# Retention outputs by features: centred values as stationary operand, and a group norm from a spread sum of squares

## The chip, the cores and the metric

The kernel runs on one core of one Trainium2 chip, as one launch. The metric is the time of that core on the device in microseconds (us), here the median of three runs. TensorE (PE in the rows; PEld is its weight load) multiplies, VectorE (DVE) and ScalarE (ACT) work on single elements, GpSimd (POOL) and SyncE (SP) mostly issue transfers. Each engine works through its own queue in order and waits for the others by semaphores.

## The reference, cut to what matters

A trunk of 4 layers is applied to 256 prompt frames and 64 sample frames, in float32. Each layer is FFN, token mixer, FFN. The mixer of layers 0 and 3 is retention, with 4 heads, 256 features of query and key and 512 of value per head. Per chunk of 64 frames:

```python
inner = einsum('bhid,bhjd->bhij', qc, kc) * decay
o = einsum('bhij,bhje->bhie', inner, vc) + einsum('bhid,bhde->bhie', qc * q_dec, s)
s = s * c_dec + einsum('bhjd,bhje->bhde', kc * k_dec, vc)
...
mu = mean(o, axis=-1)
var = mean(square(o - mu), axis=-1)
o = (o - mu) * rsqrt(var + EPS) * gn_g
y = (silu(g) * o) @ w_out
```

The final state of both sequences is an output. Only the sample has a state to begin with; the prompt's 256 frames are taken in one triangular product here, without a state.

## The kernel before, in words

**Weights and clock of the program.** All weights stream from memory as [128, 1024] chunks of eight [128, 128] tiles. ScalarE makes the high part of a chunk (`hi`, L274) and VectorE the low part (`lo`, L281), three chunks ahead of use; each tile is then used by three TensorE products of 320 or 322 columns (L375 to L377, the main products). Everything else is woven in by ticks: a tick comes every four tiles, that is every 12 main products. `at(delay, f)` records the work of `f` that many ticks later, and a heap keeps the order. A chunk border is every second tick, and `split_hi` is recorded at a border ahead of the work of that tick. So the order on every engine is fixed when the program is built.

**A head of retention** (L650 to L810) takes 24 ticks: two columns each of q, k, v, v, g, g, eight tiles a column. `normed` (L590) takes a pair of columns out of the products' memory on VectorE, `shifted` (L596) adds the shift on ScalarE, `rotate` (L668 to L673) turns q and k. Then come steps between the weight tiles: `k_rows` (L685) and `v_rows` (L696) turn k and v to rows of tokens, `scores` (L705) multiplies k by q, `attend` (L721) multiplies three tiles of tokens with 512 columns of values, the sample's with the state `s0` and 64 rows of tokens; `bn_stats` and `bn_aggr` read mean and variance there. `group_norm` waits for the three, makes 1/sqrt and scales the rows on ScalarE (`on`, L736). `gate` (L743, L747) turns a tile of 128 features back to features by tokens, multiplies by the gate and the gain and splits the product into two parts (L401, L402). `state_prompt` (L754, L756) and `state_sample` (L764, L767) make the new states, which leave on POOL's queue through three `st` buffers; on the same queue, behind them, the next head's state is loaded (L782).

**Pools that set waits.** The steps share three banks of TensorE's output memory (`wk`), taken in turn. `wide` has two buffers. The mixer's output projection (`out_projection`, L807 on) takes 16 operands; its first four outputs take the first nine operands (`RET_EARLY`) before the rest. Each output that is done is added to x by VectorE (`residual`, L555), which then prepares the next sub-layer's operand (L496, L502, L508, L513). The output banks are two tiles of two banks; output 4 takes the tile of outputs 0 and 2, so that it waits for both residuals.

Between the retention heads VectorE also works on the modulation vectors (`junk`, L472, two products of 1.2 us for a unit), by a plan that is not changed.

Of the kernel before, what the change touches and what calls it, by code (L numbers as in the profile page):

```python
# [19 lines left out]
P = 128  # L20
# [5 lines left out]
TOKT = ((0, 128), (128, 256), (256, 320))  # L26
NB = NT + 2
# [18 lines left out]
# Work on the modulation vectors per chunk of weights: row tiles on the tensor engine at a time, and units that the  # L46
# vector engine takes (before and in a sub-layer's output projection; in a retention head, by chunk).
# [4 lines left out]
# Chunks that are split ahead, buffers.  # L52
# [13 lines left out]
def sub_tiles(kind, layer):  # L66
    """[128, 128] weight tiles of a sub-layer, (weight, index, row tile, first column), as they are used."""
# [92 lines left out]
def ada_layout(subs):  # L160
    """Vector -> which engine computes it."""
# [3 lines left out]
class Consts:  # L165
    """Columns of the array of constants."""
# [25 lines left out]
def tables():  # L192
# [12 lines left out]
                   g[:, :, 0] ** np.maximum(63 - np.arange(P)[:, None], 0)], axis=2) / 16.0  # L205
# [5 lines left out]
def windows():  # L211
    """[rows, windows, tokens out]: trailing means less the frame, for the three row tiles of a projection."""
# [19 lines left out]
class Stream:  # L232
    """Weights in the order of their use: loaded ahead, split into two float32r parts ahead."""
# [76 lines left out]
class Kernel:  # L310
# [75 lines left out]
    def four_banks(self):  # L386
        """Neighbours are in different tiles."""
# [9 lines left out]
    def parts(self, src):  # L397
        """Two float32r parts of a [128, 320] operand."""
# [6 lines left out]
    def parts_later(self, src, done):  # L405
        """The same, the second part a tick later."""
# [10 lines left out]
    def rsqrt(self, m, n):  # L417
        """1 / sqrt(m) of a [128, n] operand in full float32."""
# [13 lines left out]
    def at(self, delay, f):  # L432
        """Traces f between the weight tiles, `delay` ticks of four tiles from now."""
# [58 lines left out]
    def operand_hi(self, n, t):  # L492
        """Tile t of x times the gain of sub-layer n, in two parts."""
# [27 lines left out]
    def rstd(self, cols):  # L521
        """1 / rms of the tokens, by tokens, for three sets of 128 columns."""
# [7 lines left out]
    def begin(self):  # L530
        """Queues the norm of the sub-layer that starts."""
# [54 lines left out]
    def normed(self, ps):  # L586
        """Two projections with the norm of the tokens; the shifts' part is in the last two columns."""
# [48 lines left out]
    def retention(self, n, layer):  # L636
        nc, a, j = self.nc, self.a, layer // 3
        with self.tc.tile_pool(name=f"ret{n}", bufs=2) as rp:
            y1 = [None] * (4 * RH)
            self.begin()  # L640
            for h in range(RH):
                self.retention_head(rp, j, h, y1)
# [563 lines left out]
```

## Time and profile before

| what | value |
|---|---|
| median of three runs | 2764.23 us (2763.4 to 2764.54) |
| profiled execution, span from its first to its last instruction | 2763.1 us |
| what the runs have beyond that span | 1.1 us |
| busy: TensorE, VectorE, ScalarE | 99 %, 77 %, 48 % |
| granted TensorE clock, mean | 0.999 |
| retention of layer 0, main products by L375 to L377 with what is woven in | about 278 to 577 us |
| retention of layer 3 | about 2225 to 2523 us |

The span is the time from the first to the last instruction of one execution. Busy time is a union of intervals; products of TensorE overlap in the records, so that the time which one of them takes away from the queue is the distance between starts, and not its duration. A row of a timeline gives the start and the length of a run of equal instructions, a row of groups the mean of one.

### The profile page before, as it was taken

Reading aid. Unit: us, or ns where it says so; the run is one execution under the profiler, and the core shown is the slowest. Engines: PE = TensorE matmul, PEld = TensorE weight load, DVE = VectorE, ACT = ScalarE, POOL = GpSimd, SP = SyncE. Lnnn points to the kernel's source line nnn. Section 1 sums busy time; section 2 is a strip of 40 time slices with the busy share of each in tenths; the row PEclk is TensorE's granted clock in tenths of the full one; section 3 lists DMA queues with packets and bytes.
Section 4 is the critical chain, followed back from the end, with each engine's and each line's share of the span. In section 5 each row is a group of like instructions: output and inputs, shape, how many; then the busy total and the mean of one; then the engine's idle time right before and its main releaser. Section 6 shows DMA issues by size and latency. Waiting matters only on the chain. (4 is left out here: it accounts for less than half of the span.)

```text
span 2763.1 us, 46811 instructions
## 1 busy us (share of the span) xinstructions
PE 2730.5 (99%) x18328; PEld 2614.3 (95%) x18328; DVE 2129.9 (77%) x3614; ACT 1335.3 (48%) x2409; POOL 63.7 (2%) x117
## 2 busy tenths in 40 slices
PE   7999999999999999999999999999999999999999
PEld 5999988899999998999999988999999998889999
DVE  5888777788888888889788776788888877756553
ACT  4554444445535544554454455555455445444552
POOL 0000000000000002000000021000000000000000
PEclk9999999999999999999999999999999999999999
DMA  8667454566666674667566543466666654444442
GB/s 329 234 220 243 169 177 158 205 216 216 218 223 214 211 234 161 226 217 238 193 218 224 198 154 118 167 214 211 224 203 210 226 178 166 165 141 153 150 151 94
DMA packets 149852, 543.63 MB, mean 197 GB/s; under 512 B 17744, under 2 KB 19024, under 8 KB 149376
## 3 DMA queue, kind: packets, MB, share of 16 engines
q1 hardware_dynamic: 142272, 517.51, 54.8%
q0 software_dynamic: 6208, 21.82, 2.3%
q8 instruction: 144, 2.36, 0.4%
q10 hardware_dynamic: 1152, 1.31, 0.1%
q14 instruction: 76, 0.62, 0.1%
HBM read 528.13 MB, written 12.44 MB: 196 GB/s over the span
## 5 line engine op out<-in xcount | busy, mean ns | idle before, releaser
L375 PE MATMUL mm<-xh,hi 128*128 128x322 f32 x3776 | 1196.6, 317 | 3.0 <-DVE xt L555 1.2
L377 PE MATMUL mm<-xh,lo 128*128 128x322 f32 x3776 | 1174.8, 311 | 0.0
L376 PE MATMUL mm<-xl,hi 128*128 128x322 f32 x3776 | 1171.5, 310 | 0.1
L274 ACT ACTIVATE hi<-raw 128x1024 fp32r<-128x1024 f32 x690 | 727.2, 1057 | 760.5 <-PE mm L376 652.2
L281 DVE TENSOR_TENSOR lo<-raw,hi 128x1024 fp32r<-128x1024 f32 x690 | 840.8, 1222 | 251.1 <-ACT hi L274 239.2
L375 PEld LDWEIGHTS mm<-xh,hi 128*128 128x128 f32 x3776 | 713.7, 189 | 32.9 <-issue 25.0
L376 PEld LDWEIGHTS mm<-xl,hi 128*128 128x128 f32 x3776 | 713.7, 189 | 3.2 <-issue 2.9
L377 PEld LDWEIGHTS mm<-xh,lo 128*128 128x128 f32 x3776 | 710.3, 188 | 0.0
L472 DVE SCALAR_TENSOR_TENSOR junk<-raw,cb 128x1024 f32<-128x1024 f32 x480 | 586.4, 1222 | 8.6
L375 PE MATMUL mm<-part,hi 128*128 128x320 f32 x1728 | 539.4, 312 | 1.9 <-DVE xt L555 1.9
L376 PE MATMUL mm<-part,hi 128*128 128x320 f32 x1728 | 536.7, 311 | 0.1
L377 PE MATMUL mm<-part,lo 128*128 128x320 f32 x1728 | 536.4, 310 | 0.0
L596 ACT ACTIVATE twin<-twin 128x256 f32<-128x256 f32 (+1 forms) x944 | 328.9, 419 | 184.8 <-DVE twin L590 184.5
L375 PEld LDWEIGHTS mm<-part,hi 128*128 128x128 f32 x1728 | 327.5, 190 | 8.9 <-issue 4.9
L376 PEld LDWEIGHTS mm<-part,hi 128*128 128x128 f32 x1728 | 325.6, 188 | 1.3 <-issue 1.0
L377 PEld LDWEIGHTS mm<-part,lo 128*128 128x128 f32 x1728 | 325.6, 188 | 0.0
L590 DVE TENSOR_TENSOR twin<-mm,rx 128x644 f32<-128x644 f32 (+1 forms) x240 | 195.2, 814 | 85.0 <-PE mm L377 84.5
L496 ACT ACTIVATE xh<-xt,mod 128x256 fp32r<-128x256 f32 x192 | 71.2, 421 | 197.7 <-DVE xt L555 196.1
L555 DVE SCALAR_TENSOR_TENSOR xt<-mm,mod,xt 128x256 f32<-128x256 f32 (+1 forms) x176 | 59.3, 378 | 62.5 <-PE mm L377 62.4
L409 ACT ACTIVATE part<-twin 128x320 fp32r<-128x320 f32 x176 | 81.2, 461 | 48.0 <-DVE twin L611 48.0
L611 DVE TENSOR_TENSOR twin<-twin 128x320 f32<-128x320 f32 x176 | 85.9, 491 | 23.2 <-ACT twin L596 18.7
L412 DVE TENSOR_TENSOR part<-twin,part 128x320 fp32r<-128x320 f32 x176 | 85.5, 486 | 1.1 <-ACT part L409 1.1
(165 smaller groups left out, 1146.8 us busy)
## 6 DMA issues: line engine op xcount, KB each, us to landing
raw<-in_wmain SPq DMA_DIRECT2D x690, 512.0 KB, 3.7
raw<-in_wada SPq DMA_DIRECT2D x288, 512.0 KB, 4.2
out_ret_p<-st POOLq DMA_DIRECT2D x16, 256.0 KB, 2.3
out_ret_s<-st POOLq DMA_DIRECT2D x16, 256.0 KB, 3.9
s<-in_s POOLq DMA_DIRECT2D x6, 512.0 KB, 7.0
fb<-in_fb POOLq DMA_DIRECT2D x8, 384.0 KB, 4.2
xt<-in_xt SPq DMA_DIRECT2D x1, 1280.0 KB, 11.3
fs<-in_fs POOLq DMA_DIRECT2D x8, 160.0 KB, 3.4
```

The source lines that it names most:

```text
L274: self.nc.scalar.activation(out=hi, in_=t, func=AF.Copy)
L281: self.nc.vector.tensor_tensor(out=lo, in0=t, in1=hi.bitcast(F32), op=ALU.subtract)
L375: t.matmul(out=out, lhsT=hi, rhs=xh, start=start, stop=False)
L376: t.matmul(out=out, lhsT=hi, rhs=xl, start=False, stop=False)
L377: t.matmul(out=out, lhsT=lo, rhs=xh, start=False, stop=stop)
L409: self.nc.scalar.activation(out=hi, in_=src, func=AF.Copy)
L412: self.nc.vector.tensor_tensor(out=lo, in0=src, in1=hi.bitcast(F32), op=ALU.subtract)
L472: nc.vector.scalar_tensor_tensor(out=self.junk, in0=t, scalar=1.0, in1=self.cb[:, s], op0=ALU.mult, op1=ALU.mult, accum_out=self.modv[v][: ...
L496: self.nc.scalar.activation(out=self.xh[:, t, b:e], in_=self.x[:, t, b:e], func=AF.Copy, scale=g[:, t, s:s + 1])
L590: self.nc.vector.tensor_tensor(out=t, in0=ps[:, :, 0:NB], in1=self.rx[:, None, 0:NB].to_broadcast([P, n, NB]), op=ALU.mult)
L596: self.nc.scalar.activation(out=t[:, b:e], in_=t[:, b:e], func=func, bias=t[:, NT + s:NT + s + 1])
L611: nc.vector.tensor_tensor(out=u, in0=u, in1=g, op=ALU.mult)
```

## The change

The step `attend` now runs over four tiles of 128 features and not over three tiles of tokens. The values, less their mean over the head's 512 features, are the stationary operand (`vc`, one buffer for all heads), as is the state, less its mean (`s0`, in place); the scores are the moving one. Means are taken from the sums that a ScalarE copy gives beside its output (`accum_out`), and ScalarE subtracts them (`centre`): for three tiles of v and two of the state per head. The output comes by features, with mean zero over a head, so that it is not turned back: `on`, the twelve transposes of `gate` and `bn_stats` go. ScalarE copies each output into the tile of v and squares it; VectorE adds the four squares; `stats` sums over the partitions with three products of one column and makes 1/sqrt; `spread` lays it over all partitions with three products; `gate` multiplies by gain and gate, `norm` by the spread factor, and the product is split into two parts as before. The sample's tokens are taken as the last 64 of a full tile of 128 (`FULLT`), the upper half of `vc` for it is zeroed once. The sample's new state gets its mean back: one small ScalarE operation and one of 512 columns per half.

The delays have names now; `RET_EARLY` goes from 9 to 12, the `st` buffers from 3 to 2. Comments were removed; those lines are left out.

```diff
-RET_DELAYS = (7, 8, 8, 4, 5, 8, 13, 2, 18, 14, 2, 20)
+RET_DELAYS = {"k01": 7, "scores": 8, "k2": 8, "state": 3, "v": 4, "attend": 8, "stats": 13, "spread": 16, "gate": 12,
+              "norm": 17, "prompt": (14, 16), "prompt_last": (19, 20), "sample": 20}
...
-RET_EARLY, ATT_EARLY = (9,), (4,)
+RET_EARLY, ATT_EARLY = (12,), (4,)
...
+        def centre(out, src, r, sums, c):
+
+            nc.scalar.activation(out=sums[r, c + 3:c + 4], in_=sums[r, c:c + 1], func=AF.Copy, scale=-1.0 / RDV)
+            nc.scalar.activation(out=out, in_=src, func=AF.Identity, bias=sums[r, c + 3:c + 4])
...
-            for b, e, o in halves(t):
-                nc.scalar.activation(out=vt[o:o + e, t, :], in_=ps[b:e, :], func=AF.Copy)
+                nc.tensor.transpose(out=ps[:, P * i:P * i + P], in_=v[i][:, b:e], identity=self.ident)
+            r = slice(0, P) if t < 2 else slice(NS, P)
+            nc.scalar.activation(out=vt[r, t, :], in_=ps[r, :], func=AF.Copy, accum_out=vm[r, t:t + 1])
+            if t == 2:
+                nc.scalar.activation(out=vt[0:NS, t, :], in_=ps[r, :], func=AF.Copy)
+            centre(vc[r, t, :], vt[r, t, :], r, vm, t)
+
+        def centre_state():
+            for d in range(2):
+                nc.scalar.activation(out=s0[:, d], in_=s0[:, d], func=AF.Copy, accum_out=sm[:, d:d + 1])
+                centre(s0[:, d], s0[:, d], slice(0, P), sm, d)
...
-            for i, (w, x) in enumerate(pairs):
-                nc.tensor.matmul(out=ps[0:r, :], lhsT=w, rhs=x, start=i == 0, stop=i == len(pairs) - 1)
...
+            c = slice(P * i, P * i + P)
+            for b, e, w, x, first, final in ((0, 256, vc[:, 0, c], sd[:, 0:256], True, False),
+                                             (128, 256, vc[:, 1, c], sd[:, 256:384], False, True),
+                                             (256, 320, s0[:, 0, c], qd[:, 0], True, False),
+                                             (256, 320, s0[:, 1, c], qd[:, 1], False, False),
+                                             (256, 320, vc[:, 2, c], sd[:, 384:448], False, True)):
+                nc.tensor.matmul(out=ps[:, b:e], lhsT=w, rhs=x, start=first, stop=final)
+            nc.scalar.activation(out=v[i][:, 0:NT], in_=ps[:, 0:NT], func=AF.Copy)
+            sq = gs if i == 0 else self.single("osq")
+            nc.scalar.activation(out=sq, in_=ps[:, 0:NT], func=AF.Square)
+            if i:
+                nc.vector.tensor_tensor(out=gs, in0=gs, in1=sq, op=ALU.add)
...
+        def stats():
+            ps = wk()
+            for t, (b, e) in enumerate(FULLT):
+                nc.tensor.matmul(out=ps[:, t:t + 1], lhsT=gs[:, b:e], rhs=self.ones, start=True, stop=True)
...
+        def spread():
             ps = wk()
...
+                nc.tensor.matmul(out=ps[:, b:e], lhsT=st["y"][:, t:t + 1].to_broadcast([P, P]),
+                                 rhs=self.ident[:, o:o + e - b], start=True, stop=True)
+            nc.vector.tensor_copy(out=rs, in_=ps[:, 0:NT])
...
+        def norm(i):
             y = self.single("y")
...
+            nc.vector.tensor_tensor(out=y, in0=v[i][:, 0:NT], in1=rs, op=ALU.mult)
             y1[4 * h + i] = self.parts(y)
...
+                nc.scalar.activation(out=st, in_=st, func=AF.Identity, bias=sm[:, d:d + 1])
```

The order on TensorE, in the second head of layer 0. Before, the products of `attend` for the last tile of tokens (`s` is the state, `sd` and `qd` the scores and queries):

```order
2187 L377 MATMUL mm<-xh,lo 128x322
2188 L721 MATMUL wk<-s_3646,qd 64x512 x2
2189 L721 MATMUL wk<-vt,sd 64x512
2190 L375 MATMUL mm<-xh,hi 128x322
2191 L376 MATMUL mm<-xl,hi 128x322
```

Now one of the four steps of `attend` there:

```order
2204 L379 MATMUL mm<-xh,lo 128x322
2205 L744 MATMUL wk<-sd,vc 128x256
2206 L744 MATMUL wk<-sd,vc 128x128
2207 L744 MATMUL wk<-qd,s_3677 128x64 x2
2208 L744 MATMUL wk<-sd,vc 128x64
2209 L377 MATMUL mm<-xh,hi 128x322
```

Six products of 512 columns in three steps became twenty of 64 to 256 columns in four; the last of each step needs the third tile of `vc`.

The order on ScalarE in the same head, from the last chunk border ahead of the turning of v (`hi` is the split of a weight chunk, `twin` the shift of a column). Before:

```order
282 L274 ACTIVATE hi<-raw 128x1024
283 L698 ACTIVATE vt<-wk 128x512
284 L274 ACTIVATE hi<-raw 128x1024
285 L698 ACTIVATE vt<-wk 128x512
286 L596 ACTIVATE twin<-twin 128x256
287 L596 ACTIVATE twin<-twin 128x64
```

Now, up to the second tile of v (`sm` and `vm` hold sums and means):

```order
302 L276 ACTIVATE hi<-raw 128x1024
303 L721 ACTIVATE s_3677,sm<-s_3677 128x512
304 L705 ACTIVATE sm<-sm 128x1
305 L706 ACTIVATE s_3677<-s_3677,sm 128x512
306 L721 ACTIVATE s_3677,sm<-s_3677 128x512
307 L705 ACTIVATE sm<-sm 128x1
308 L706 ACTIVATE s_3677<-s_3677,sm 128x512
309 L714 ACTIVATE vt,vm<-wk 128x512
310 L705 ACTIVATE vm<-vm 128x1
311 L706 ACTIVATE vc<-vt,vm 128x512
```

Six operations on the state stand ahead of v, and each tile of v has two operations more, the last one of which writes what `attend` needs.

The order on ScalarE from the first prompt state of the head before to the border behind the sample's state. Before, the parts (`part`) and the states (`st`) of a head were spread over ten ticks:

```order
257 L756 ACTIVATE st<-wk 128x512
258 L274 ACTIVATE hi<-raw 128x1024
259 L401 ACTIVATE part<-y 128x320
260 L756 ACTIVATE st<-wk 128x512
261 L274 ACTIVATE hi<-raw 128x1024
262 L401 ACTIVATE part<-y 128x320
```

Now:

```order
279 L276 ACTIVATE hi<-raw 128x1024
280 L403 ACTIVATE part<-y 128x320 x2
281 L598 ACTIVATE twin<-twin 128x256
282 L598 ACTIVATE twin<-twin 128x64
283 L598 ACTIVATE twin<-twin 128x256
284 L598 ACTIVATE twin<-twin 128x64
285 L403 ACTIVATE part<-y 128x320 x2
286 L276 ACTIVATE hi<-raw 128x1024
287 L792 ACTIVATE sm<-sm 128x2
288 L796 ACTIVATE st<-st,sm 128x512 x2
289 L276 ACTIVATE hi<-raw 128x1024
```

The four parts stand in two ticks behind a border, and the sample's states, which take VectorE's result, stand ahead of the next border's `hi`.

## Rows read from the trace of the kernel before

**Rows 1.** The head of the page: span, and busy time of each engine with its share of the span and its instructions.

```profile
span 2763.1 us, 46811 instructions
PE 2730.5 (99%) x18328; PEld 2614.3 (95%) x18328; DVE 2129.9 (77%) x3614; ACT 1335.3 (48%) x2409; POOL 63.7 (2%) x117
```

**Rows 2.** Busy time by stretch, for the two retentions: length of the stretch, busy us of PE, PEld, DVE, ACT, POOL, then granted clock, DMA share, GB/s.

```profile
278.00:576.70 298.70, 298.70 (x1850) 263.80 (x1849) 224.44 (x421) 142.21 (x253) 11.49 (x21) 1.00 0.53 182
2225.00:2523.00 298.00, 298.00 (x1833) 265.54 (x1832) 204.47 (x382) 143.08 (x254) 10.26 (x19) 1.00 0.46 159
```

**Rows 3.** Timeline of TensorE in the first head: start us, length us, instruction. The first step of `attend` with a step of `v_rows` right behind it; then the third step of `attend`, and a `gate`, each with the main product ahead of it; and always the second main product behind.

```profile
319.10 1.02 PE L721 MATMUL wk<-vt,sd 128*128 128x512 f32 x2
319.95 0.60 PE L696 MATMUL wk<-cst,twin 128*128 128x128 f32 x4
...
320.54 0.30 PE L376 MATMUL mm<-xl,hi 128*128 128x322 f32 x1
...
325.94 0.30 PE L377 MATMUL mm<-xh,lo 128*128 128x322 f32 x1
326.18 1.93 PE L721 MATMUL wk<-s,qd 128*64 128x512 f32 x4
...
329.29 0.32 PE L376 MATMUL mm<-xl,hi 128*128 128x322 f32 x1
...
339.71 0.31 PE L377 MATMUL mm<-xh,lo 128*128 128x322 f32 x1
339.86 0.58 PE L743 MATMUL wk<-cst,on 128*128 128x128 f32 x3
...
340.62 0.30 PE L376 MATMUL mm<-xl,hi 128*128 128x322 f32 x1
```

**Rows 4.** The same timeline at the norm of the sub-layer (three products of one column, two records each).

```profile
285.43 0.30 PE L377 MATMUL mm<-xh,lo 128*128 128x322 f32 x1
285.58 0.72 PE L525 MATMUL stat<-cst,acc 128*128 128x1 f32 x6
...
286.39 0.31 PE L376 MATMUL mm<-xl,hi 128*128 128x322 f32 x1
```

**Rows 5.** Groups of ScalarE's instructions by line and shape: count, busy us, mean ns of one, then idle time ahead of them and what ended it.

```profile
L274 ACT ACTIVATE hi<-raw 128x1024 fp32r<-128x1024 f32 x690 | 727.2, 1057 | 760.5 <-PE mm L376 652.2 <-issue 56.3 <-ACT hi L274 15.9
L596 ACT ACTIVATE twin<-twin 128x256 f32<-128x256 f32 x472 | 237.4, 503 | 184.8 <-DVE twin L590 184.5
...
L401 ACT ACTIVATE part<-y 128x320 fp32r<-128x320 f32 x32 | 15.1, 472 | 55.5 <-DVE y L747 55.1
...
L698 ACT ACTIVATE vt<-wk 128x512 f32<-128x512 f32 x16 | 9.6, 598 | 13.6 <-PE wk L696 13.6
...
L990 ACT ACTIVATION_READ_ACCUMULATOR pr<-pr,nm 128x1 f32 x40 | 7.5, 188 | 0.0
...
L518 ACT ACTIVATE xh<-mod 128x16 fp32r<-128x16 f32 x12 | 2.5, 205 | 7.5 <-DVE mod L482 3.8 <-PE pm L376 3.7
```

**Rows 6.** Timeline of ScalarE in the second head, and TensorE's first turning of v there.

```profile
370.91 1.06 ACT L274 ACTIVATE hi<-raw 128x1024 fp32r<-128x1024 f32 x1 [0.72 <-ACT kd L689]
371.87 1.38 ACT L596 ACTIVATE twin<-twin 128x256 f32<-128x256 f32 x4
374.47 1.06 ACT L274 ACTIVATE hi<-raw 128x1024 fp32r<-128x1024 f32 x1 [1.21 <-issue]
...
376.16 0.60 PE L696 MATMUL wk<-cst,twin 128*128 128x128 f32 x4
```

**Rows 7.** Timeline of VectorE behind the second head: the low part of an operand, the evacuation of a pair of columns, and the first `lo` behind the rotation that follows it, with the instruction after that.

```profile
402.36 0.50 DVE L402 TENSOR_TENSOR part<-y,part 128x320 fp32r<-128x320 f32 x1 [0.54 <-ACT part L401]
402.77 0.82 DVE L590 TENSOR_TENSOR twin<-mm,rx 128x644 f32<-128x644 f32 x1
...
407.32 1.22 DVE L281 TENSOR_TENSOR lo<-raw,hi 128x1024 fp32r<-128x1024 f32 x1
408.45 0.54 DVE L747 SCALAR_TENSOR_TENSOR y<-wk,vecs,twin 128x320 f32<-128x320 f32 x1
```

**Rows 8.** Timeline of VectorE in the output projection of layer 0 (residuals L555 of outputs 0 to 2, the sample's states L767, a unit on the modulation vectors), and the first product of output 4 on TensorE; from the page, the prompt's states: KB each, us from issue to landing.

```profile
537.27 0.68 DVE L555 SCALAR_TENSOR_TENSOR xt<-mm,mod,xt 128x256 f32<-128x256 f32 x2 [2.57 <-PE mm L377]
...
539.00 1.28 DVE L767 SCALAR_TENSOR_TENSOR st<-s,wk 128x512 f32<-128x512 f32 x2
...
540.79 1.22 DVE L472 SCALAR_TENSOR_TENSOR junk<-raw,cb 128x1024 f32<-128x1024 f32 x1
...
545.91 0.67 DVE L555 SCALAR_TENSOR_TENSOR xt<-mm,mod,xt 128x256 f32<-128x256 f32 x2
...
547.59 0.31 PE L375 MATMUL mm<-part,hi 128*128 128x320 f32 x1
...
out_ret_p<-st POOLq DMA_DIRECT2D x16, 256.0 KB, 2.3
```

**Rows 9.** Busy time by stretch, for the two longest stops of TensorE outside the start and what followed them; columns as in Rows 2.

```profile
1066.60:1068.60 2.00, 0.08 (x2) 0.04 (x1) 1.00 (x2) 1.91 (x4) 2.00 (x4) 1.00 0.59 190
1068.60:1072.60 4.00, 4.00 (x26) 3.75 (x27) 3.28 (x9) 1.59 (x5) 2.04 (x4) 1.00 0.09 36
...
1733.80:1735.90 2.10, 0.16 (x2) 0.10 (x1) 1.91 (x6) 0.31 (x1) 0.00 (x0) 1.00 0.48 187
1736.00:1739.40 3.40, 3.40 (x14) 3.40 (x14) 3.27 (x8) 2.75 (x7) 0.00 (x0) 0.50 0.45 154
```

More of the change, by code (lines that the diff above doesn't have):

```diff
@@ L651, in retention_head @@
         qd = rp.tile([P, 2, NS], F32, tag="qd", name="qd", bufs=1)
-        mv = self.small.tile([P, 3, 2], F32, tag="mv", name="mv")
+        gs = rp.tile([P, NT], F32, tag="gs", name="gs", bufs=1)
+        rs = rp.tile([P, NT], F32, tag="rs", name="rs", bufs=1)
+        vm = self.small.tile([P, 6], F32, tag="vm", name="vm")
+        sm = self.small.tile([P, 6], F32, tag="sm", name="sm")
+        st = {}
         def wk():
@@ L717, in attend @@
             ps = wk()
-            pairs = (((sd[:, 0:128], vt[:, 0]),), ((sd[:, 128:256], vt[:, 0]), (sd[:, 256:384], vt[:, 1])),
-                     ((qd[:, 0], s0[:, 0]), (qd[:, 1], s0[:, 1]), (sd[0:NS, 384:448], vt[0:NS, 2])))[t]
-            for i, (w, x) in enumerate(pairs):
-                nc.tensor.matmul(out=ps[0:r, :], lhsT=w, rhs=x, start=i == 0, stop=i == len(pairs) - 1)
-            o.append(ps)
-            st = self.small.tile([P, 6], F32, tag="bn", name="bn")
-            nc.vector.bn_stats(out=st[0:r], in_=ps[0:r, :])
@@ L725, in attend @@
-            nc.vector.bn_aggr(out=mv[0:r, t, :], in_=st[0:r])
-        def group_norm():
-            m = self.small.tile([P, 3], F32, tag="gnm", name="gnm")
-            nc.vector.tensor_scalar(out=m, in0=mv[:, :, 1], scalar1=EPS, scalar2=None, op0=ALU.add)
-            y = self.rsqrt(m, 3)
-            nb = self.small.tile([P, 3], F32, tag="gnb", name="gnb")
-            nc.vector.scalar_tensor_tensor(out=nb, in0=mv[:, :, 0], scalar=-1.0, in1=y, op0=ALU.mult, op1=ALU.mult)
-            for t, (b, e) in enumerate(TOKT):
-                r = e - b
-                u = rp.tile([P, RDV], F32, tag="on", name="on", bufs=3)
-                nc.scalar.activation(out=u[0:r], in_=o[t][0:r, :], func=AF.Identity, scale=y[0:r, t:t + 1],
-                                     bias=nb[0:r, t:t + 1])
-                on.append(u)
@@ L745, in gate @@
+        def gate(i):
             c = 16 * j + 4 * h + i
+            nc.vector.scalar_tensor_tensor(out=v[i][:, 0:NT], in0=v[i][:, 0:NT], scalar=self.vecs[:, c:c + 1],
+                                           in1=g[i][:, 0:NT], op0=ALU.mult, op1=ALU.mult)
+        def norm(i):
             y = self.single("y")
-            nc.vector.scalar_tensor_tensor(out=y, in0=ps[:, 0:NT], scalar=self.vecs[:, c:c + 1], in1=g[i][:, 0:NT],
-                                           op0=ALU.mult, op1=ALU.mult)
+            nc.vector.tensor_tensor(out=y, in0=v[i][:, 0:NT], in1=rs, op=ALU.mult)
@@ L787, in retention_head @@
             self.after_norm(1, lambda z=z: rotate(z))
-        self.at(RET_DELAYS[0], lambda: k_rows((0, 1)))
-        self.at(RET_DELAYS[1], scores)
-        self.at(RET_DELAYS[2], lambda: k_rows((2,)))
+        self.at(RET_DELAYS["k01"], lambda: k_rows((0, 1)))
+        self.at(RET_DELAYS["scores"], scores)
+        self.at(RET_DELAYS["k2"], lambda: k_rows((2,)))
         for _ in range(2):
             columns(lambda ps: linear(ps, v))
+        self.at(RET_DELAYS["state"], centre_state)
         for t in range(3):
-            self.at(RET_DELAYS[3] + t, lambda t=t: v_rows(t))
-            self.at(RET_DELAYS[4] + t, lambda t=t: attend(t))
-        self.at(RET_DELAYS[5], group_norm)
-        last = h == RH - 1
+            self.at(RET_DELAYS["v"] + t, lambda t=t: v_rows(t))
         for i in range(4):
-            self.at(RET_DELAYS[6] + (1 if last else RET_DELAYS[7]) * i, lambda i=i: gate(i))
-        for d in range(2):
-            self.at(RET_DELAYS[8] + d if last else RET_DELAYS[9] + RET_DELAYS[10] * d, lambda d=d: state_prompt(d))
-        self.at(RET_DELAYS[11], state_sample)
+            self.at(RET_DELAYS["attend"] + i, lambda i=i: attend(i))
+            self.at(RET_DELAYS["gate"] + i, lambda i=i: gate(i))
+            self.at(RET_DELAYS["norm"] + i // 2, lambda i=i: norm(i))
+        self.at(RET_DELAYS["stats"], stats)
+        self.at(RET_DELAYS["spread"], spread)
+        for d, delay in enumerate(RET_DELAYS["prompt_last" if h == RH - 1 else "prompt"]):
+            self.at(delay, lambda d=d: state_prompt(d))
+        self.at(RET_DELAYS["sample"], state_sample)
         for _ in range(2):
```

51 lines of the change are left out of this document (25 added, 26 removed).

## The prediction

> **What bounds the kernel.** I read the page's head first: TensorE is busy 2730.5 of 2763.1 us, VectorE 77 %, ScalarE 48 % [rows 1]. Then the stretches of the two retentions: TensorE busy 298.7 of 298.7 us and 298.0 of 298.0 us, full clock [rows 2]. So it never stops there, whatever the others wait for; in these 597 us the time is the sum of what TensorE issues. Two things can move it: what a step costs TensorE, and a new wait that stops it.
>
> A step's price is the start of the second main product behind it, less the start of the one ahead, less two main steps of 0.148 us (285.43 to 285.58 shows one [rows 4]).
>
> **What TensorE loses, per head.** The first `attend` is one product of 512 columns: 319.10 to 319.95, 0.85 [rows 3]. The second has two, 1.70. The third, three products with 64 columns or rows on a side, takes 329.29 - 325.94 - 0.30 = 3.05. A `gate` takes 340.62 - 339.71 - 0.30 = 0.61, four 2.46 [rows 3]. Sum removed: 8.06.
>
> **What it gains, per head.** Three products of one column take 286.39 - 285.43 - 0.30 = 0.66, so 0.22 each, set by weights and not by columns [rows 4]. I price products of up to 128 columns so and one of 256 at half of 0.85, 0.43. An `attend` step is then 0.43 + 4 x 0.22 = 1.31, four 5.25; `stats` 0.66, `spread` 0.66. Sum added: 6.57. The turning of k and v and the scores keep their columns, and a side of 128 for 64 costs nothing in the first step's transposes (320.54 - 319.95 - 0.15 = 0.44 for four [rows 3]). Net -1.49 per head, **-11.9 us** for eight. Bounds: by columns alone a product of 64 takes 0.85 / 8 = 0.11, twelve of them save 1.4 a head more, -23; if each step paid what the third step of `attend` has over three plain products (3.05 - 2.55 = 0.5), four pay 2.0 more, and the sum is +4. I take -11.9, since rows 4 have the same 128 x 128 weights.
>
> The Trainium skill ("TensorE: Matmul & The Clock Gate", Back-to-back issue gap) gives about 60 cycles for a lone product of up to 64 columns and 134 for 128, and says beside it that load and product together set the spacing. By the table alone the sum would lie near the -23; rows 4 show 0.11 us per record even for one column, so the measurement decides.
>
> **What ScalarE and VectorE gain.** A 512-column operation on ScalarE out of SBUF has no row; between 472 ns for 320 and 1057 for 1024 the slope is 0.83 ns a column, which gives 0.63 us. A bias adds 0.08 (256 columns take 503 ns with one, 0.42 by the slope): 0.72. A sum read beside a copy lengthens it by half of the 188 ns; a small one takes 0.20; neighbours overlap by 0.09 (a `hi` of 1.06 is followed after 0.96 [rows 6]), while a dependent one waits for the end and 0.03 more [rows 5]. Centring one tile is copy with sum, small operation, subtraction: 1.57 us from the turned v (598 ns copy), 1.60 for a half of the state, 2.12 for the third v tile with its second copy. One estimate for all: 10 % either way.
>
> The skill ("ScalarE: Activation LUTs", Rules for kernel authors) wants additions on VectorE and not on ScalarE, which speaks against five subtractions here; two-tensor work of 320 columns takes VectorE 0.50 [rows 7], so the trace agrees, though VectorE is the busier engine.
>
> **The path that decides: from the last head's `norm` to the next `attend`.** Ticks count from a head's first tile; the next v is turned at tick 44, `norm` falls on border 33. Times from that border. TensorE: ten ticks of 1.78, the sample's state (two products side by side, between 0.85 and 1.70: 1.25), k 0.44 and scores 0.85 + 4 x 0.22 + 0.22 = 1.96 bring border 43 to 21.4; one more tick, three turnings of v at 0.44 and four ticks bring the first `attend` to 31.6, and its last product, which needs the third `vc`, to **32.7**.
>
> Now the others, by the order quoted above. ScalarE's `hi` of border 33 is done at 1.05, and the first `part` stands behind it. Two norms (multiply 0.49, `part` 0.47, low part 0.41, two handovers) end at 3.4. Evacuation of k and its rotation take 407.32 - 402.77 = 4.55, a `lo` 1.13 [rows 7]: 9.1. The next two norms, 1.43 each: the last `part` ends at 11.5. Only then ScalarE does `hi` of border 35, ends at 12.5; `lo` until 13.6. VectorE's two operations on the sample's state (1.28 [rows 8]) end at 14.3 and 14.9. ScalarE adds the mean, 0.72 each, until 15.7; it has held border 37's `hi` back all that time: ends 16.6. Shift of v 1.29, `hi` of border 39 ends at 18.9; VectorE's `lo` waits for it, ends at 20.0; score factors 1.0, evacuation of the second v pair 0.82 [rows 7]: 21.9. Shift 1.29: ScalarE comes to border 43 at 23.2, and TensorE was there at 21.4. From here `hi` 0.96, state 3.2, v 1.57, `hi` 0.96, v 1.57, shift of g 1.29, third v 2.12: **34.8**. TensorE waits 34.8 - 32.7 = 2.1 and loads weights, 2.2 us, with all main products behind it in its queue. Before, ScalarE came to that border idle: a 1.21 gap, then `hi` at 374.47, 1.69 ahead of TensorE's 376.16 [rows 6]. In a layer's first head nothing came before, and 34.8 - 1.7 leaves 0.5. So per layer 0.5 + 3 x 2.2 = 7.1, **+14.2** for both. Bounds: 10 % on the 34.8 steps' unmeasured part (some 12 us of centring and states) is 1.2 either way per head, 1.0 to 3.4: +6 to +21. Below nothing it can't go, since no main product becomes shorter.
>
> **The output projection.** Output 4 needs residual 2. Before, that ended at 546.6, and output 4 began at 547.59 [rows 8]. Now the first four outputs take 12 operands first, so that outputs 0 to 2 end 12, 8 and 4 tiles ahead of output 4, that is 5.3, 3.6 and 1.8 us. From the projection's start TensorE gets there at 64 x 0.444 + 2.6 + 1.3 + 4.7 = 37.0. In layer 0 VectorE, behind the squares, 1/sqrt, four `lo` and two units on the modulation vectors (2.4 each [rows 8]), begins `norm` at about 20.9 and ends the fourth at 27.9; ScalarE comes to the first prompt state at 28.1 behind the parts, stores it at 28.7; it lands at 31.0 (2.3 [rows 8]). The sample's state waits for that buffer, since only two are left: until 32.5. A unit 2.4, residual 0.67, `lo` 1.14, operand 0.67, residual 0.67, operand and squares 1.7, residual 0.67: 40.5. TensorE waits 3.5. Layer 3 has no units there; the same sum gives 37.6, a wait of 0.6. Together **+4.1**, between 0 (stores land early, VectorE 5 us ahead of this sum) and +8.
>
> **The clock.** Of the two longest stops, 2 us each, one was followed by 3.4 us at clock 0.5, the lower of the two levels, and one was not [rows 9]. 3.4 us at half rate give away up to 1.7. Seven stops of 2 us or more: 0 to +12. I take one, **+1.7**, since most stops of my sum are barely as long as these two.
>
> Every edit that lies beside TensorE I cost at nothing: the other squares, sums, `rs` and gates end two us or more ahead of their use by the same sums. The next head's load of the state stands on POOL behind the sample's stores, now one ScalarE operation later, but has its whole v pair to land.
>
> **Sum.** 2763.1 - 11.9 + 14.2 + 4.1 + 1.7 = 2771.2 us of span. The runs have 1.1 more than the profiled span: **2772** against the median of 2764.2. About 0.2 %, 5.5 us, is what a measurement can tell from no change.
>
> **Rivals.** (a) ScalarE is back in time: the handovers between norms, states and shifts are shorter than summed and border 43 finds it idle, as rows 6 show before. Then each head waits 0.5, the projections 0 to 4: 2764.2 - 11.9 + 4 + 2 = 2758, faster by 0.2 %. For it: 48 % busy [rows 1]. Against: the queue is in order, and its new work stands in one place. It decides when the chain of 34.8 is 1.7 shorter. (b) No wait at all, or products by columns: 2764.2 - 11.9 = 2752, down to 2741. Against: the on-time sum still ends behind TensorE. (c) The clock falls at each stop: 2772 + 6 x 1.7 = 2782; rows 9 show one of two. (d) Each `attend` step pays 0.5 for its changes of shape, as the third does now: the saving goes, 2772 + 16 = 2788; all sides are 128 now, which speaks against it. (e) Half of the lateness, a wait of 1.2: 2772 - 6 = 2766, no change.
>
> **Chances.** Forecast 0.45 (2766 to 2780 by itself), (a) 0.22, (b) 0.08, (c) 0.11, (d) 0.04, (e) 0.10. Faster: (b) and half of (a), 0.2. Same: half of (a), (e), a tenth of the forecast's cases: 0.27. Slower: 0.53. The range that leaves out two in ten reaches from inside (a) to (c): 2755 to 2783.
>
> **What would show it.** `attend` steps of 1.3 us where they don't wait, no `gate` on TensorE. In each head but a layer's first, TensorE's idle time ahead of the last product of the first `attend`, ended by ScalarE's `vc`, some 2 us; `hi` late at borders 35 to 43. A wait of output 4 for VectorE in layer 0. Idle states at border 43, or TensorE as busy as in rows 2, would prove the forecast wrong; so would `attend` steps far from 1.3.

## The result and the profile after

The changed kernel takes 2784.43 us, the median of four runs (2781.27 to 2785.68), beside 2763.82 of the kernel before, run with it. The ratio is 1.0069, with a 95 % interval of 1.0056 to 1.0081: 0.7 % slower. The forecast was 2772, the range 2755 to 2783: the kernel became slower, as forecast, but by 20.6 us and not by 8, and the median lies 1.4 us above the upper end of the range.

The head of the page after, to be read against [rows 1]:

```profile
span 2783.4 us, 47547 instructions
PE 2733.0 (98%) x18552; PEld 2651.9 (95%) x18552; DVE 2137.9 (77%) x3614; ACT 1401.6 (50%) x2609; POOL 64.5 (2%) x119
```

The span is 20.3 us longer and TensorE is busy almost as long as before. That hides two things, which the stretches of the two retentions show (the columns are those of [rows 2]; the stretches are longer because the layers are). The last two lines are 3.4 us behind the second head's first attend step, and the stop in the third head's:

```profile
278.00:583.00 305.00, 295.30 (x1925) 277.85 (x1924) 224.69 (x413) 172.44 (x348) 11.49 (x21) 0.98 0.52 175
2225.00:2533.00 308.00, 298.78 (x1946) 283.73 (x1945) 212.51 (x391) 176.24 (x355) 10.26 (x19) 0.98 0.48 158
...
388.10:391.50 3.40, 3.40 (x15) 3.21 (x14) 1.23 (x1) 1.82 (x3) 0.00 (x0) 0.50 0.58 183
447.50:449.70 2.20, 0.07 (x1) 0.00 (x0) 2.13 (x5) 2.11 (x5) 0.00 (x0) 0.97 0.62 212
```

TensorE, which never stopped there before, stands idle for 9.7 and 9.2 us. And what counts as busy is partly work at half rate: in the third line it holds 15 products where the same time at full clock holds 26 (a line further below). A busy share alone would have shown neither.

What TensorE waited for, by the waiting instruction and the one that ended the wait: total us, number of waits, longest.

```profile
PE wk L744 <- ACT vc L706: 13.9, 8, 2.2
PE mm L377 <- DVE xt L557: 7.9, 5, 3.4
...
PEld wk L729 <- DVE st L795: 1.3, 5, 0.3
...
PEld wk L790 <- ACT st L782: 0.8, 1, 0.8
```

The first line is new: the first attend step (L744) waits for ScalarE's centred v (L706) in all eight heads. Six of the eight stops are 1.7 to 2.2 us, those of the two first heads 0.2 and 1.0. In the second line 3.4 and 1.5 us belong to the two output projections; the rest was there before. The last two are waits for a bank of PSUM at the scores and at the state's products.

One such stop on TensorE and the ScalarE instructions that lead to it, second head (start us, length us, instruction):

```profile
383.51 0.31 PE L379 MATMUL mm<-xh,lo 128*128 128x322 f32 x1
383.66 0.81 PE L744 MATMUL wk<-sd,vc 128*128 128x256 f32 x4
384.31 0.56 PE L744 MATMUL wk<-qd,s 128*128 128x64 f32 x4
387.06 0.43 PE L744 MATMUL wk<-sd,vc 128*128 128x64 f32 x2 [2.20 <-ACT vc L706]
387.31 0.39 PE L377 MATMUL mm<-xh,hi 128*128 128x322 f32 x1
```

```profile
374.85 1.04 ACT L276 ACTIVATE hi<-raw 128x1024 fp32r<-128x1024 f32 x1
375.80 0.61 ACT L721 ACTIVATE s<-s 128x512 f32<-128x512 f32 x1
...
385.44 0.59 ACT L716 ACTIVATE vt<-wk 64x512 f32<-64x512 f32 x1
...
386.29 0.72 ACT L706 ACTIVATE vc<-vt,vm 64x512 f32<-64x512 f32 x1
387.04 1.06 ACT L276 ACTIVATE hi<-raw 128x1024 fp32r<-128x1024 f32 x1
```

Four of the five products of the step are issued, and only the last, which needs the third piece of v, waits from 384.9 to 387.1. On ScalarE none of these rows carries an idle time in brackets: from 374.85 on it works without a pause until the instruction that TensorE waits for. Where [rows 6] had 1.21 us of idle time there is now a queue.

The granted clock was 0.50, the lower of its two levels (1.2 of 2.4 GHz), for 3.4 us, beginning within 1.1 us of the end of five of these stops (from 388.1, 449.6, 2347.4, 2408.8 and 2470.3 us) and for 6.8 us at the stop of layer 0's output projection. The kernel before had no such stretch in its retentions; the two that both kernels have lie in other layers.

So the 20.3 us are: 13.9 at the attend steps, 4.9 at the projections, 2.1 for banks, up to 11.9 (half of 23.9 us) of clock, less about 12 saved on TensorE. These add up to 20.8 and are rougher than they look. By the prediction's price of a step, the one above takes 3.73 us where a step that doesn't wait takes 1.32, so a stop of 2.20 costs 2.41; a fall of the clock gives away nearer 1.5 than 1.7 us (experiment 1); and outside the two retentions this execution is 1.2 us shorter than the one before.

### The profile page after: what moved, and what is told of

The parts are those of the page before. It is cut to its first block, busy times and chain, and to the rows that moved or that the text cites. A ratio compares the mean times of both kernels' runs of the same rounds, so it can differ in the third digit from the quotient of the medians.

```text
span 2783.4 us, 47547 instructions
## 1 busy us (share of the span) xinstructions
PE 2733.0 (98%) x18552; PEld 2651.9 (95%) x18552; DVE 2137.9 (77%) x3614; ACT 1401.6 (50%) x2609; POOL 64.5 (2%) x119
## 3 DMA queue, kind: packets, MB, share of 16 engines
q10 hardware_dynamic: 1152, 1.31, 0.1%
## 5 line engine op out<-in xcount | busy, mean ns | idle before, releaser
L613 DVE TENSOR_TENSOR twin<-twin 128x320 f32<-128x320 f32 x176 | 85.9, 491 | 23.2 <-ACT twin L598 18.7
L557 DVE SCALAR_TENSOR_TENSOR xt<-mm,mod,xt 128x256 f32<-128x256 f32 (+1 forms) x176 | 59.3, 378 | 51.8 <-PE mm L379 51.7
```

Of the source, the lines that this page charges most:

```text
L613: nc.vector.tensor_tensor(out=u, in0=u, in1=g, op=ALU.mult)
```

## The experiments

Theory A: ScalarE is late with the third piece of centred v, partly from work brought along from the border of the heads, partly from what the change put just ahead; every long stop then costs more through the clock. The rivals are named with each run.

**1. Fill the stop.** In heads 1 to 3:

```diff
                 nc.tensor.matmul(out=ps[:, b:e], lhsT=w, rhs=x, start=first, stop=final)
+                if i == 0 and h > 0 and b == 128:
+                    for _ in range(9):
+                        nc.tensor.matmul(out=ps[:, 320:448], lhsT=vc[:, 0, c], rhs=sd[:, 0:128], start=True, stop=True)
```

> In heads 1 to 3 of each retention layer nine extra products of 128 columns (0.22 us each, 1.98 us together), which nobody reads, stand in the first attend step ahead of the products that wait for the third piece of centred v. TensorE then works through most of the stop of 2.2 us; the stop itself is no shorter, since the ScalarE instruction that ends it isn't touched. Theory A (the stops are 2.2 us of waiting, and each one that is followed by a granted clock of 0.50 for 3.4 us costs another 1.7): the idle time ahead of the fifth product falls from 2.2 to about 0.2, the step ends when it ended before, the five falls of the clock behind these stops are gone, and the time falls by 5 x 1.7 = 8.5 us to about 2776. Rival C (the clock falls in the retention heads for another reason than the stop, the new mix of products for one): the clock falls as before, and the time stays at 2784 to 2785.

Measured 2777.11 us, 7.3 less than the changed kernel. The filling products, then the stretch behind the same stop as above, and the waits that are left:

```profile
385.43 2.17 PE L747 MATMUL wk<-sd,vc 128*128 128x128 f32 x18
...
387.40:391.00 3.60, 3.42 (x26) 3.23 (x25) 2.85 (x5) 3.21 (x5) 0.00 (x0) 1.00 0.68 221
```

```profile
PE wk L744 <- ACT vc L706: 2.1, 7, 1.0
```

The head is no faster at the place itself; TensorE only has something to do there. The clock stays at 1.00 behind all of these steps, and the one fall left in the retentions is at the projection's stop of 2.8 us, which wasn't filled. Five falls less for 7.3 us is 1.5 us each, near the 1.7 that half of 3.4 gives. (Between the same main products, which come in the same order in every kernel, the heads themselves are 7.5 us shorter in this trace; elsewhere 2.7 us less and 2.6 more cancel.) So the clock follows the stops, and rival C (another reason for the falls) goes.

**2. Leave out the centring of the state.**

```diff
-                nc.scalar.activation(out=s0[:, d], in_=s0[:, d], func=AF.Copy, accum_out=sm[:, d:d + 1])
-                centre(s0[:, d], s0[:, d], slice(0, P), sm, d)
+                nc.vector.memset(sm[:, d:d + 1], 0.0)
+                nc.vector.memset(sm[:, d + 3:d + 4], 0.0)
```

> Leaves out the centring of the sample's state (the two sums and the two shifted copies on ScalarE; the state goes uncentred into the outputs): ScalarE loses about 3.2 us per head just ahead of the three pieces of v. Theory A (ScalarE is late at that place): the third piece of centred v comes up to 3.2 us sooner, the stops ahead of the first attend step go from 13.9 us in all to under 0.5, the six falls of the clock in the retention layers go with them except the one at the output projection (1.7 us of cost each, four or five of them), and the time falls by 13.5 + 8.5 = 22 us to about 2762. Rival B (not the work put in by the change but the attend step's own order or the turning of v on TensorE sets the stop): the stops stay at 2.2 us and the time within 2 us of 2784.

Measured 2760.62 us, a ratio of 0.9985 (0.9976 to 0.9995) to the kernel before. No stop of over 0.5 us is left at any attend step, and the clock doesn't fall in the retentions. The attend step and v are as they were, so rival B in this form falls.

**3. The sample's state later, so that ScalarE doesn't wait for it.**

```diff
-        self.at(12, load_state)
+        self.at(14, load_state)
...
-        self.at(RET_DELAYS["sample"], state_sample)
+        self.at(RET_DELAYS["sample"] + (2 if h < RH - 1 else 0), state_sample)
```

> The step that forms the sample's new state is taken two ticks (3.6 us) later in heads 0 to 2, and the load of the next head's state with it; no work is added or left out. ScalarE then has the turned projections and a weight chunk to do in the 1.85 us in which it stood idle for VectorE ahead of the new state. Theory A (it is a lateness carried from the border of the heads that makes ScalarE late for the third piece of v): the stops of heads 1 to 3 go from 2.2 to between 0.4 and 1.5 us, the clock does not fall behind stops of that size (it didn't behind those of 1.7 and 1.0 us in the trace), and the time falls by 5 to 9 us of stops and 5 x 1.7 us of clock, to about 2770. Rival B (only the work put just ahead of the attend step counts, 3.2 us of state and 5.7 us of v per head, whatever was late before): the stops stay at 2.2 us and the time at 2784.

Measured 2781.0 us, 3.4 less instead of 14. Its waits, and ScalarE just ahead of the state's centring:

```profile
PE wk L729 <- DVE st L795: 10.3, 6, 1.9
PE mm L377 <- DVE xt L557: 8.1, 5, 3.0
PE wk L744 <- ACT vc L706: 6.3, 8, 1.0
```

```profile
377.31 1.06 ACT L276 ACTIVATE hi<-raw 128x1024 fp32r<-128x1024 f32 x1 [1.18 <-PE mm L378]
378.28 0.61 ACT L721 ACTIVATE s<-s 128x512 f32<-128x512 f32 x1
```

The stops at the attend step did shrink, to 0.85 us in heads 1 to 3, but 10.3 us came up at the scores. The two products of the sample's state hold two of the three banks until VectorE has read them; at the later tick the scores need those banks. I had not seen that wait coming. The run is still useful: ScalarE was idle for 1.18 us just ahead of the centring, so it brought no lateness along, and TensorE nevertheless stopped for 0.85. That suggests a split of the 2.2 us: some 0.9 from the work on the spot, some 1.3 from lateness. (TensorE itself came later to that place, by its stop of 1.85 us at the scores, so experiment 8 takes the split up again.) Neither the forecast's rival "on time: 0.5" nor "all on the spot" has it.

**4. The last head's new state in place of the old, without a staging buffer.**

```diff
-                st = rp.tile([P, RDV], F32, tag="st", name="st", bufs=2)
+                st = s0[:, d] if h == RH - 1 else rp.tile([P, RDV], F32, tag="st", name="st", bufs=2)
```

> In the last head the new state of the sample is written in place of the old one, so it needs no staging buffer, and VectorE doesn't wait for the two stores of the prompt's state (3.65 and 1.25 us of VectorE idle time in layer 0) ahead of the residual that sets a bank free. Theory A (the stop of 3.4 us at the fifth output of layer 0 comes from that wait, and its two falls of the clock, 6.8 us at half speed, from the stop): the stop goes to under 0.5 us, the clock stays up there, the stop of 1.5 us in layer 3 goes too, and the time falls by 3.4 + 3.4 + 1.5 = 8 us to about 2776. Rival D (the residual is late on VectorE for its own reasons, the unit of the modulation vectors and the chain of norms ahead of it): the stop shrinks by less than half, and the time falls by under 3 us.

First VectorE in the changed kernel, then in this run, in layer 0's output projection: the sample's state (L795) and the residuals (L557).

```profile
547.45 0.69 DVE L795 SCALAR_TENSOR_TENSOR st<-s,wk 128x512 f32<-128x512 f32 x1 [3.65 <-DMA out_ret_p<-st]
549.39 0.69 DVE L795 SCALAR_TENSOR_TENSOR st<-s,wk 128x512 f32<-128x512 f32 x1 [1.25 <-DMA out_ret_p<-st]
...
552.40 0.67 DVE L557 SCALAR_TENSOR_TENSOR xt<-mm,mod,xt 128x256 f32<-128x256 f32 x2
```

```profile
543.78 1.28 DVE L795 SCALAR_TENSOR_TENSOR s<-s,wk 128x512 f32<-128x512 f32 x2
...
548.02 0.68 DVE L557 SCALAR_TENSOR_TENSOR xt<-mm,mod,xt 128x256 f32<-128x256 f32 x2 [0.55 <-PE mm L379]
```

Measured 2774.08 us, 10.3 less. The two brackets "<-DMA out_ret_p" are the waits for the prompt's stores. Without them the first residual starts 4.4 us sooner and waits for TensorE (its bracket) instead of holding it up; no stop of over 0.5 us is left in either projection. The heads' stops are untouched (13.8 us), with four falls behind them instead of five: 4.9 of stops, up to 3.4 of clock at the projection and 1.7 in the heads make 10.0. Rival D, by which VectorE is late there for its own reasons, falls. The expectation had one thing wrong, as the prediction had: the product that waits is not the fifth output's first but the third output's thirteenth (56 tiles into the projection; in layer 3 the fourth output's, 60 tiles in). The third output shares a buffer with the first, so it waits for residual 0, that is for the row at 552.40.

**5. The state's work where ScalarE has time.** Nothing is left out:

```diff
-              "norm": 17, "prompt": (14, 16), "prompt_last": (19, 20), "sample": 20}
+              "norm": 17, "prompt": (16, 18), "prompt_last": (19, 20), "sample": 13}
...
-        self.at(12, load_state)
+        self.at(8, load_state)
+        self.at(12, centre_state)
...
-        self.at(RET_DELAYS["state"], centre_state)
```

> All the work of the change stays. The sample's new state is formed seven ticks sooner (right behind the head's last attend step, where ScalarE stands idle for about 2.6 of 3.6 us), the next state's load goes from tick 12 to 8, its centring from tick 19 to 12 (again a stretch in which ScalarE was idle), and the two products for the prompt's state two ticks later. The 3.2 us of state centring and the 1.85 us of waiting are then no longer ahead of the three pieces of v on ScalarE. Theory A (order on ScalarE's queue, not its amount of work, makes the stops): all the stops ahead of the first attend step are under 0.5 us, the sample's state is done well ahead of the output projection so that its residual isn't held up by stores (3.4 and 1.5 us of stops there go to under 1.5 together), no clock falls in the heads, and the time is the 2784.4 of the changed kernel less 13.4 less 8.5 less about 7: 2755 to 2758, below the 2764 of the kernel before. Rival B (ScalarE's added 11 us per head don't fit whatever their order): stops of 1 to 2 us turn up elsewhere, at the scores or the state products, and the time stays above 2770. Rival E (the new products are dearer than they look, so that the change loses even with no stop): no stops, but the time at 2764 or above.

Measured 2753.12 us, the median of five runs and 2 us below the range expected, a ratio of 0.9965 (0.9952 to 0.9979) to the kernel before: 0.35 % faster than it, and 31 us less than the changed kernel. The stretches of the retentions, and the same 3.4 us as above:

```profile
278.00:583.00 305.00, 304.57 (x2041) 289.25 (x2040) 236.59 (x442) 179.64 (x359) 11.48 (x21) 1.00 0.56 186
2225.00:2533.00 308.00, 307.92 (x2053) 295.13 (x2053) 218.02 (x406) 184.40 (x368) 10.26 (x19) 1.00 0.47 159
...
388.10:391.50 3.40, 3.40 (x26) 3.35 (x25) 2.36 (x3) 2.10 (x7) 0.00 (x0) 1.00 0.80 271
```

TensorE is again busy in all of them, at full clock. The second head's third piece of v, and TensorE's load of weights for the product that takes it:

```profile
383.50 0.72 ACT L706 ACTIVATE vc<-vt,vm 64x512 f32<-64x512 f32 x1
```

```profile
384.27 0.30 PEld L744 LDWEIGHTS wk<-sd,vc 128*128 128x128 f32 x2 [0.17 <-ACT vc L706]
```

It comes just too late: the products' row shows no idle time, but the load waits 0.17 us, and the first attend step takes 1.55 to 1.60 us instead of 1.32 in the second and third heads of both layers, 1.0 us together. The profiled span is 2751.1, 12.0 under [rows 1]; the medians, with 2763.38 for the kernel before run beside it, are 10.3 apart. Between the same main products (those that start at 278 and 583, 2225 and 2533 us in the changed kernel) the two retentions take 580.6 us, 591.6 in the kernel before and 613.0 in the changed one; the rest of the 12.0 lies in other layers. So the saving on TensorE is 11.0, or 12.0 without the four short waits, and rivals B (ScalarE's work doesn't fit in any order) and E (the new products are dear) fall. What moving the centring alone would give, with the sample's state left where it was, wasn't run.

**6. The attend step later.**

```diff
+        late = 2 if h < RH - 1 else 0
         for i in range(4):
-            self.at(RET_DELAYS["attend"] + i, lambda i=i: attend(i))
+            self.at(RET_DELAYS["attend"] + late + i, lambda i=i: attend(i))
...
```

(and so for gate, norm, statistics and spread)

> Attend, statistics, spread, gate and norm of heads 0 to 2 come two ticks (3.6 us) later; nothing is added or left out, and the last head stays as it is. ScalarE's order ahead of the third piece of v is the same, but it has 3.6 us more. Theory A: the stops of heads 0 to 2 (0.2, 2.2, 2.2 and 1.0, 2.2, 2.2 us) are gone with their four falls of the clock, those of the last heads (1.7 and 2.2) stay or grow by up to 2 us, since the norms of the head before now come two ticks later on ScalarE and VectorE; the time falls by 10 + 6.8, less up to 4: 2768 to 2772. Rival B (ScalarE's whole queue shifts along with the attend step, since its work per head is what is too much): the stops come back two ticks later at the same size, and the time stays at 2782 or above.

```profile
PE mm L377 <- DVE xt L557: 7.5, 5, 3.0
PE wk L744 <- ACT vc L706: 3.6, 2, 2.2
```

Measured 2765.11 us, 19.3 less, where 2768 to 2772 was expected. Two waits for v are left, those of the last heads, 1.4 and 2.2 us; they did not grow. The wait doesn't follow the attend step to its later place, so it is a matter of when, and rival B falls again. With the projections' stops still in it the kernel stands level with the one before (0.9995 to 1.0013).

**7. One copy behind the centring instead of ahead of it.**

```diff
-            if t == 2:
-                nc.scalar.activation(out=vt[0:NS, t, :], in_=ps[r, :], func=AF.Copy)
             centre(vc[r, t, :], vt[r, t, :], r, vm, t)
+            if t == 2:
+                nc.scalar.activation(out=vt[0:NS, t, :], in_=ps[r, :], func=AF.Copy)
```

> Only the order of two ScalarE instructions in the turning of v's third piece is changed: the copy of its 64 rows to the other half (0.59 us) comes behind the centring instead of ahead of it. Theory A (the stop ends with this chain of ScalarE instructions): each of the eight stops is 0.6 us shorter, from 2.2 to 1.6 and from 1.7 to 1.1, 4.4 us together; behind a stop of this size the clock fell in about one case of three (1.69 us: once of two; 1.85 us: twice of five), so some three of the five falls go, another 5 us: 2775 to 2780, with the lower end if none is left. Rival F (the fall of the clock comes with any stop over a microsecond): 4.4 us of stops less, the falls all there: 2780. Rival B (another chain sets the stop): 2784.

```profile
PE wk L744 <- ACT vc L706: 9.4, 7, 1.6
```

Measured 2773.7 us, 10.7 less, for the order of two instructions; 2775 to 2780 was expected. The stops fell by 4.5 us, to 1.6 (five) and 1.1; the clock fell behind two of the 1.6 ones instead of five. With 1.5 to 1.7 us for each of the three, and 3.4 us less at half clock at the projection (which the expectation didn't have), that is the measured gain within 1 us. Rival F (a fall behind every stop of over a microsecond) is wrong: three stops of 1.6 had none.

**8. Experiment 5 with the centring back in its place.**

```diff
-        self.at(12, centre_state)
+        self.at(19, centre_state)
```

> The same as e5_state_early but for one number: the state's centring goes back from tick 12 to 19, just ahead of the three pieces of v. So the lateness that ScalarE brought along from the border of the heads is taken away as in that run, and the 3.2 us of centring stand where the change put them. In e3_sample_later ScalarE stood idle for 1.2 us just ahead of the centring, so it wasn't late there, and TensorE still stopped for 0.85 us at the attend step. Theory A, made finer by that trace (2.2 us of stop = 0.85 from the work put between tick 19 and the attend step, 1.35 from lateness brought along): the stops are 0.8 to 1.0 us in seven heads and 0.2 in the first, 6 us in all, no clock falls behind them, and the time is that of e5_state_early plus 6: 2759. Rival A' (lateness is all of it): no stops, 2753 to 2754. Rival B (the work on the spot is all of it): stops of 2.2 us, falls of the clock behind most, 2770 to 2775.

```profile
PE wk L744 <- ACT vc L706: 6.8, 8, 1.0
```

Measured 2760.33 us, 7.2 more than experiment 5. Seven stops of 0.90 to 0.99 us, no fall of the clock in the retentions. This is the split that experiment 3 suggested, now without its stops at the scores: about 0.9 us belongs to the centring where the change put it, and the rest of the 2.2 to the lateness carried from the border.

## Where the prediction was right, and where it was off

**The saving on TensorE** was right. Forecast 11.9 us; experiment 5, in which little else stands in the way, has retentions shorter by 11.0, or 12.0 without its four short waits. An attend step takes 1.32 us (forecast 1.31) and the statistics 0.67 (0.66), from the start of the second main product less that of the first and two main steps of 0.15:

```profile
339.68 0.31 PE L379 MATMUL mm<-xh,lo 128*128 128x322 f32 x1
339.83 0.72 PE L754 MATMUL wk<-cst,gs 128*128 128x1 f32 x6
340.42 0.39 PE L377 MATMUL mm<-xh,hi 128*128 128x322 f32 x1
340.65 0.30 PE L378 MATMUL mm<-xl,hi 128*128 128x322 f32 x1
```

(340.65 - 339.68 - 0.30 = 0.67.) That a product of one to 128 columns costs 0.22 held, so the price by columns in rival (b) and the price of changed shapes in rival (d) are both out.

**The stops in the heads** were right in place, cause and size: forecast 14.2 us, measured 13.9, six of eight near 2. The chain was right too. Counted from the border at which the forecast starts (31.6 us before the attend step at 383.66), the last `part` ends at 11.1 (forecast 11.5), the sample's state at 15.4 (15.7), ScalarE comes to border 43 at 22.8 (23.2), and the third piece of v is done at 35.0 (34.8). The last two hide a small piece of luck: ScalarE came 0.4 us sooner, and its work from there on took 12.2 us instead of 11.6. ScalarE's estimated prices held:

```profile
L706 ACT ACTIVATE s<-s,sm 128x512 f32<-128x512 f32 x16 | 11.6, 724 | 0.5
...
L721 ACT ACTIVATE s<-s 128x512 f32<-128x512 f32 x16 | 9.8, 615 | 0.0
...
L705 ACT ACTIVATE sm<-sm 128x1 f32<-128x1 f32 x16 | 3.2, 203 | 0.5
```

(forecast 0.72, 0.63 and 0.20 us). Two readings beside these prices were weak. The 0.03 us behind a dependent instruction stands in no row of [rows 5]; the changed kernel shows it (a small operation from 376.54 to 376.74, the next at 376.77). And VectorE's 0.50 for 320 columns [rows 7] is no faster than ScalarE's 0.47 for a copy of as many [rows 5]; at 512 columns it is 0.69 (L795) beside ScalarE's 0.72, so the agreement noted there is thin. The split within the sum was a little off: without lateness the forecast had 0.5 us left; experiments 3 and 8 show 0.85 to 0.97. Experiment 8, in which ScalarE starts that border's `hi` 1.3 us sooner (at 373.57, not 374.85), is close to rival (a) as a run: 2760, where the rival had 2758.

**The output projection** had the right size in layer 0 (forecast 3.5 us, measured 3.4) and the right cause: with the wait for the stores gone (experiment 4) the stop goes too. But two errors cancel in it. "Output 4 needs residual 2" is not what holds TensorE up; output 2 needs residual 0, some 8 tiles sooner for TensorE and 5 us sooner for VectorE. By the forecast's own sum that would have been a wait of about 2 (TensorE there at 33.5, residual 0 done at 35.6). And the stores that VectorE waits for land later than [rows 8] had them. The page after, then the two stores of this projection after and before:

```profile
out_ret_p<-st POOLq DMA_DIRECT2D x16, 256.0 KB, 4.1
...
out_ret_p<-st POOLq DMA_DIRECT2D x2, 256.0 KB, 4.7
...
out_ret_p<-st POOLq DMA_DIRECT2D x2, 256.0 KB, 3.8
```

The 2.3 us was a median of all sixteen; the two at this place took 3.8 in the kernel before already, so it was the wrong price from the start. Why they are slower still now is open. The two now start 0.5 us apart, and 3.5 before, but in other heads of the changed kernel the second store starts 5.3 us behind the first and still takes 4.3 to 5.2. In layer 3 the stop was 1.5 instead of 0.6. Two waits for banks were not in the sum: 1.3 us at the scores, 0.8 at the state's products in layer 0.

**The clock** is the term that was mis-sized, and with it the forecast: 1.7 us, one fall of seven possible. There were five falls behind the six stops of 1.7 to 2.2 us in the heads, and a double one at layer 0's projection: up to 11.9 us. Experiment 1 measures the five in the heads at 7.3. The forecast's own rival (c), 2782, priced it; I gave it too little because one of the two stops in [rows 9] showed no fall. Even those odds, one of two, would have made some 6 us of seven stops. I took one fall because most stops were "barely as long as these two", of 1.92 and 1.94 us, against my own sum, which had 2.1 to 2.2 for the six in the heads. The ten traces together show how poor that sample was: the pooling layer's stop of 1.92 us, the same in all ten, was followed by a fall in five, the attention projection's of 1.95 in two, the retention's of 2.2 in nine of eleven.

2772 plus 10.2 for the clock, 2.1 for the banks and 0.8 at the projections, less 0.4 for the heads and the saving, is 2784.7; measured 2784.4. That it meets so closely is partly luck: the stops stand in it without the 0.2 us that each costs beyond its idle time, and the clock at its upper bound. Experiment 1 gives 7.3 to 7.5 for the five falls, and experiment 4 some 2.5 for the double one (in its trace layer 0's projection is 6.1 us shorter, of which the stop is 3.4 to 3.6): some 10 in all.

## What to carry to other kernels

Where one engine is always busy, price a new wait by where the waited-for instruction stands in its engine's queue, and look for a stretch in which that engine is idle: here the same 31 us of difference, from 0.7 % slower to 0.35 % faster, came from moving two pieces of work, the state's centring and the sample's new state, seven ticks ahead, and the prompt's two back. A stop of 2.2 us on TensorE here cost its length and, in nine of eleven cases, a clock at half rate behind it (the stops of 1.9 us in other layers in seven of twenty); filling it, or shortening it by half a microsecond, is worth trying even where the wait itself stays. When a step is moved, list the PSUM banks and staging buffers that it holds, and who asks for them at the new place.

## What the runs showed of the hardware that was not expected

In these layers the granted clock fell the more often behind a stop, the longer the stop was, and not in every execution for the same stop. Stops of TensorE in the retention layers, counted over the traces of both kernels and the eight experiments, with the number that had a stretch at 0.50 beginning within 2 us of their end:

```
length of the stop, us    stops    followed by clock 0.50
0.84 to 0.99                17          0
1.08 to 1.54                10          0
1.58 to 1.85                12          5
2.17 to 2.20                11          9
2.83 to 3.41                 6          5
```

Single cases cut both ways: a stop of 1.69 us had a fall in one run and none in another, and one of 3.2 us (experiment 2, layer 0's projection) had none. These counts are of this kernel's mix of work; in other layers the stops of 1.92 us had a fall in five of ten, those of 1.95 in two. Nor is a stop's length the whole of it: in the attention layer, at about 1600 us, the clock fell in seven of the ten traces where the longest stop just ahead was 1.3 us. In two of the seven (experiments 3 and 4) it was 0.4 us. What decides is open. It wasn't tried.
